# Weight sums of the seven-product pairs: made ahead and parked in DRAM, for 46 pairs instead of 33

## The chip, the cores and the metric

The kernel runs on one core of a Trainium2 chip. A core has TensorE (PE: matmuls; its weight loads are shown apart as PEld), VectorE (DVE), ScalarE (ACT), GpSimd (POOL) and SyncE (SP); DMA engines move data between DRAM and the on-chip memory, on queues that SP, ACT and POOL issue to. The metric is the device time of one execution in microseconds; lower is better.

## The reference

A trunk of two layers works on x of shape (1, 256, 2048) in float32: a gated linear attention layer, then a layer of block-sparse attention (with 256 positions and blocks of 256 each position sees its own block alone), and behind each a gated feed-forward block with a short convolution. The part around the change is the feed-forward block:

```python
def conv_ffn(x, norm_w, w_up, conv_w, conv_b, w_down):
    S = x.shape[1]
    h = rms_norm(x, norm_w) @ w_up                   # (256, 2048) @ (2048, 11264)
    hp = jnp.pad(h, ((0, 0), (CONV_WIDTH - 1, 0), (0, 0)))
    acc = conv_b
    for j in range(CONV_WIDTH):
        acc = acc + conv_w[j] * hp[:, j:j + S]
    a, u = jnp.split(acc, 2, axis=-1)
    return (jax.nn.silu(a) * u) @ w_down             # (256, 5632) @ (5632, 2048)

def reference(x, ...):
    h = x
    for layer in range(DEPTH):                       # 2
        h = h + (gla_mixer(h, ...) if layer < 1 else moba_mixer(h, ..., *shared_kv(h, ...)))
        h = h + conv_ffn(h, ...)
    return h
```

## The kernel before

**Products in three parts.** Matmuls run in a reduced float32 format. To keep the accuracy, every operand is split into a high part (a rounding copy by ACT, line 127 for weights) and a low part (the difference, by DVE, line 128), and a product is three matmuls: high x high, low x high, high x low.

**The weight stream.** `WeightStream` (lines 55 to 140) feeds all weights in the order in which they are used: chunks of 128 x 2048 float32 (1 MB) come by SP's queue into the pool `raw` (3 tiles, `wraw`), and each chunk is split in halves of 1024 columns (`whi`, `wlo`). Of four halves three live in the pool `parts` (3 tiles each) and, in most stages, the fourth in two *slots*. A slot is 4 KB per partition of the pool `big` (37 of them), which also holds h, the operands of the projections, the hidden activations (`hid`, 22 slots) and the combinations below. One `step()` of the program takes one half from the stream, after it has emitted the splits of the next three (two in the attention stage) and the loads up to three chunks ahead. `after(n, job)` puts a job n steps later.

**The stages** are: GLA with its output projection (128 steps), up projection 0 (176 steps), down projection 0, the attention stage with its output projection (128 steps), up projection 1 (176 steps) and down projection 1.

**The down projection.** `down` (lines 632 to 695) works on two blocks of 1024 output columns. A block takes 22 *pairs* of 128-row slices of w_down, each a 2 x 2 arrangement of tiles (2 row slices x 2 column halves of 512), against 2 x 2 tiles of the activations (2 row slices x 2 halves of the 256 positions). A plain pair makes all eight tile products, in two steps of 12 matmuls. A *seven* pair (marked + in `ORDERS`) uses the seven-product scheme for 2 x 2 matrices (Strassen's, in Winograd's form): it needs four sums of the pair's weight tiles and four sums of its activation tiles, and makes its products in four steps of 3, 6, 6 and 6 matmuls. The results of its extra products stand in four PSUM banks of their own and are drained into the outputs once for each block by `u_sums` (lines 697 to 718). The last pairs of each block, behind the last seven pair (`_tail`, up to three), are worked column half by column half.

The sums of the weights are made on the spot: `_sums` (lines 96 to 103) runs three DVE operations (lines 100 to 102) from the raw tile into the two slots `t13` and `t24`, and these are then split like any half. The sums of the activations are made by `combine` (lines 584 to 594) into one slot for each pair: for the pairs 1, 3, 5 and 7 (`EARLY`) during the up projection, for the others by `combine_parts` at the pairs 2, 4, 6 ... of the first block that uses them, and they serve both blocks.

Layer 0's second block also has jobs: two slots of h are loaded back at pairs 0 and 1, two more at 15 and 16 (`load_back`, POOL's queue), and at the pairs 2, 2, 3 and 4 the first block's outputs are turned on PE and added to h (`back`), followed at once by the work for the next norm (`nrm.feed`).

**What sets the order.** The program is written in one order; a planner at build time then orders each engine's and queue's instructions, by priority in the written order among those that its own costs hold to be ready, and hands out the tiles of each pool as they come free. On the chip each engine and each queue runs its list in that fixed order, waiting on semaphores.

## Time and profile before

| | before |
|---|---|
| median of 3 runs | 2219.98 us (2219.92 to 2220.67) |
| the profiled execution | 2220.21 us, of which the span of its instructions is 2218.4 |
| granted TensorE clock | 1.000 |
| busy: PE / PEld / DVE / ACT / POOL | 2212.0 / 1910.7 / 1669.9 / 1259.3 / 46.8 us |
| matmuls | 11781 |
| moved by DMA | 428.50 MB, mean 193 GB/s |
| down projection 0, 1 | 876.7 to 1106 us, 1986 to 2214 us of the span |

How to read it: the span is the time from the first to the last instruction. Busy time is the union of an engine's instructions. A matmul's own duration (390 ns for 512 columns) is longer than its distance from the next one, since matmuls are pipelined, so groups of matmuls that alternate are counted with overlap; stages are better compared by windows of time and by the distance of starts. In a group's row stand its line, engine and operation, out<-in, shapes, count, busy us, mean ns of one, and the idle time of the engine just before, with what ended it. In a row of waits stand who waited, for whom, us in total, how often, and the longest.

### The profile page before, as it was taken

The numbers are of one execution on the slowest core, as the hardware profiler recorded it, in microseconds if no ns is written. First come the engines' busy times: TensorE is split into PE (matmuls) and PEld (weight loads), VectorE is DVE, ScalarE is ACT, GpSimd is POOL, SyncE is SP. The second block draws the span as 40 slices with busy tenths as digits, with TensorE's granted clock in tenths as the row PEclk, the third lists the DMA queues.
The fourth block names the chain that finished last, engine by engine and source line by source line (L and its number), as shares of the span: only waits on it lengthen the run. The fifth ranks groups of instructions, "written<-read, shape, count | busy, mean of one in ns | idle before, by whom it ended". The sixth has DMA issues, their size and how long they took to land.

```text
span 2218.4 us, 30212 instructions
## 1 busy us (share of the span) xinstructions
PE 2212.0 (100%) x11781; PEld 1910.7 (86%) x11781; DVE 1669.9 (75%) x2291; ACT 1259.3 (57%) x1758; POOL 46.8 (2%) x61
## 2 busy tenths in 40 slices
PE   9999999999999999999999999999999999999999
PEld 7889888888888888888888888888888888888887
DVE  6666776788777778978866676567787777789896
ACT  6655644665555555645556665446555555556453
POOL 0000000000000000000010000000000000000000
PEclk9999999999999999999999999999999999999999
DMA  7554455555555555565655544555555555556664
GB/s 279 177 196 140 171 201 212 195 190 190 188 186 192 186 191 183 204 228 198 219 197 203 171 155 169 190 190 200 198 188 189 185 190 187 190 186 225 224 212 152
DMA packets 63442, 428.50 MB, mean 193 GB/s; under 512 B 7569, under 2 KB 8097, under 8 KB 13250
## 3 DMA queue, kind: packets, MB, share of 16 engines
q1 hardware_dynamic: 59490, 415.43, 53.7%
q0 software_dynamic: 3232, 10.56, 1.4%
q8 instruction: 92, 1.51, 0.3%
q10 hardware_dynamic: 576, 0.58, 0.1%
q14 instruction: 52, 0.43, 0.1%
HBM read 420.23 MB, written 6.32 MB: 192 GB/s over the span
## 4 chain that ended last, share of the span: by engine, by line
PE 99%; DMA 0%; ACT 0%; DVE 0%; SPq 0%; issue 0%
PE acc L312 40%; PE acc L314 21%; PE acc L662 13%; PE acc L327 10%; PE p L662 8%; PE acc L330 5%; PE sT L517 0%; DMA wraw<-w_v 0%; PE tr L855 0%; PE s L873 0%; PE pT L893 0%; PE z L423 0%; PE s L871 0%; PE oT L403 0%; PE o L403 0%; PE hT L726 0%
## 5 line engine op out<-in xcount | busy, mean ns | idle before, releaser
L127 ACT CAST whi<-wraw 128x1024 fp32r<-128x1024 f32 (+1 forms) x786 | 798.4, 1030 | 598.1 <-PE acc L312 329.1
L128 DVE TENSOR_TENSOR wlo<-wraw,whi 128x1024 fp32r<-128x1024 f32 (+1 forms) x786 | 926.8, 1195 | 260.6 <-ACT whi L127 135.5
L312 PE MATMUL acc<-xw,whi 128*128 128x512 f32 x3328 | 796.9, 391 | 0.0
L312 PEld LDWEIGHTS acc<-xw,whi 128*128 128x128 f32 x3328 | 610.9, 188 | 118.0
L314 PEld LDWEIGHTS acc<-xw,wlo 128*128 128x128 f32 x3328 | 426.8, 191 | 16.1
L314 PE MATMUL acc<-xw,wlo 128*128 128x256 f32 x3328 | 432.6, 283 | 0.0
L662 PE MATMUL acc<-whi,hid 128*128 128x512 f32 x572 | 181.9, 390 | 0.0
L662 PE MATMUL p<-whi,hid 128*128 128x512 f32 x506 | 164.6, 389 | 0.0
L327 PE MATMUL acc<-whi,xkv 128*128 128x512 f32 x512 | 133.6, 394 | 0.0
L327 PE MATMUL acc<-whi,xw 128*128 128x512 f32 x512 | 129.7, 393 | 1.1 <-ACT whi L127 1.1
L618 DVE SCALAR_TENSOR_TENSOR au<-up,cs,au 128x255 f32<-128x255 f32 x176 | 84.6, 482 | 59.4 <-ACT au L616 58.8
L662 PEld LDWEIGHTS acc<-whi,hid 128*128 128x128 f32 x572 | 107.0, 188 | 22.0
L340 ACT COPY up<-acc 128x512 f32<-128x512 f32 x88 | 51.6, 586 | 118.5 <-PE acc L314 117.9
L327 PEld LDWEIGHTS acc<-whi,xw 128*128 128x128 f32 x512 | 95.6, 189 | 21.9 <-ACT whi L127 2.0
L127 ACT CAST whi<-t 128x1024 fp32r<-128x1024 f32 x66 | 68.9, 1054 | 77.0 <-PE p L662 61.5
L662 PEld LDWEIGHTS p<-whi,hid 128*128 128x128 f32 x506 | 95.0, 188 | 19.8
L327 PEld LDWEIGHTS acc<-whi,xkv 128*128 128x128 f32 x512 | 94.3, 188 | 18.4
L616 ACT ACTIVATE au<-up,cs 128x256 f32<-128x256 f32 x176 | 96.0, 593 | 7.8 <-DVE up L612 7.8
L662 PE MATMUL acc<-wlo,hid 128*128 128x512 f32 x286 | 94.2, 389 | 0.0
L128 DVE TENSOR_TENSOR wlo<-t,whi 128x1024 fp32r<-128x1024 f32 x66 | 79.6, 1219 | 18.1 <-PE p L662 10.0
L662 PE MATMUL acc<-whi,comb 128*128 128x512 f32 x264 | 85.5, 389 | 0.0
L662 PE MATMUL p<-wlo,hid 128*128 128x512 f32 x253 | 83.4, 389 | 0.0
(259 smaller groups left out, 2027.7 us busy)
## 6 DMA issues: line engine op xcount, KB each, us to landing
wraw<-w_up SPq DMA_DIRECT2D x176, 1024.0 KB, 4.8
wraw<-w_dn SPq DMA_DIRECT2D x88, 1024.0 KB, 4.9
wraw<-w_g SPq DMA_DIRECT2D x16, 1024.0 KB, 4.9
wraw<-w_go SPq DMA_DIRECT2D x16, 1024.0 KB, 4.9
wraw<-w_mq SPq DMA_DIRECT2D x16, 1024.0 KB, 4.9
wraw<-w_kk SPq DMA_DIRECT2D x16, 1024.0 KB, 4.8
wraw<-w_kv SPq DMA_DIRECT2D x16, 1024.0 KB, 4.9
wraw<-w_mo SPq DMA_DIRECT2D x16, 1024.0 KB, 4.9
```

What stands on the lines that cost most here:

```text
L127: nc.scalar.copy(hi[:, a:b], src[:, a:b])
L128: nc.vector.tensor_sub(lo[:, a:b], src[:, a:b], hi[:, a:b].bitcast(F32))
L312: T.matmul(ps[:, b, :], two[i][0][:, c:c + 128], xs(kt), start=kt == 0, stop=False)
L314: T.matmul(ps[:, b, :S], two[i][1][:, c:c + 128], xs(kt)[:, :S], start=False, stop=kt == kts - 1)
L327: T.matmul(ps[:, t, :], xs(kt)[:, x0 + 128 * t:x0 + 128 * t + 128], hi[:, c:c + 512], start=kt == 0 and x0 == 0, stop=False)
L330: T.matmul(ps[:, t, :], xs(kt)[:, 128 * t:128 * t + 128], lo[:, c:c + 512], start=False, stop=kt == KT - 1)
L340: A.copy(t, ps[:, :, S:])
L616: A.activation(au[:, i, :], t[:, i, :], AF.Identity, bias=col(cb + n), scale=col(cw + 2 * 2 * FT + n))
L618: V.scalar_tensor_tensor(au[:, i, 1:], t[:, i, :S - 1], col(cw + 2 * FT + n), au[:, i, 1:], op0=OP.mult, op1=OP.add)
L662: T.matmul(p[n], x[xi], w[wi][:, 512 * f:512 * f + 512], start=n not in begun, stop=left[n] == 0)
```

## The change

- **More seven pairs.** `ORDERS` marks 11, 11, 11 and 13 pairs in the four blocks instead of 8, 8, 8 and 9, in a new order. A mark is now + or ^. Of the 46 marked pairs 23 carry each mark.
- **The weight sums are made ahead.** For every marked pair `make_ahead` loads the pair's four weight tiles once (1 MB, SP's queue, into a tile of `raw`), makes the four sums in place with four DVE operations of 128 x 512, one per step, 4 to 7 steps after the load, and stores the tile to DRAM by POOL's queue 8 steps after it. Layer 0's 22 pairs are made every 12 steps from step 24 of the program, layer 1's 24 pairs every 12 steps from the eighth step of the attention stage.
- **The stream loads them back.** A marked pair is now two chunks: the last three quarters of its weight tiles (in a new order, so that the one tile that is used alone comes first), and its parked sums. The sums of a + pair come into a `raw` tile, those of a ^ pair into two slots, in two transfers. `_sums` is gone. In the down projections the stream loads five chunks ahead instead of three.
- **Memory.** `raw` has 4 tiles instead of 3, `big` 35 slots instead of 37. `combine` packs the sums of four pairs' activations into three slots (the fourth sum of each pair goes into a part of `hid` that a seven pair doesn't use), and is called one pair earlier.
- **Order.** In a seven pair the products 6 and 5 share a step, and 7 and 4. In layer 0's second block both first reloads of h stand at pair 0, `back` at the pairs 2, 2, 3, 3, and `nrm.feed` apart from it at 4, 6, 8 and 10.

```diff
@@ -37,14 +37,15 @@
 def _order(text):
-    return [(int(k.rstrip("+")), k.endswith("+")) for k in text.split()]
+    return [(int(k.rstrip("+^")), k[len(k.rstrip("+^")):]) for k in text.split()]
 EARLY = (1, 3, 5, 7)
-ORDERS = [[_order("0 2 4 1+ 6 3+ 8 5+ 10 7+ 12 16 9+ 14 11+ 17 13+ 18 15+ 19 20 21"),
-           _order("0 2 4 6 8 1+ 10 3+ 12 5+ 14 7+ 16 9+ 17 11+ 18 13+ 19 15+ 20 21")],
-          [_order("0 2 4 1+ 6 3+ 8 5+ 10 7+ 12 16 9+ 14 11+ 17 13+ 18 15+ 19 20 21"),
-           _order("0 1+ 2 3+ 4 5+ 6 7+ 8 9+ 10 11+ 12 13+ 14 15+ 16 17+ 18 19 20 21")]]
+ORDERS = [[_order("0 1+ 2 3^ 4 5+ 6 7^ 8 9+ 11^ 10 13+ 15^ 12 16+ 17^ 14 19+ 18 20 21"),
+           _order("0 2 4 6 1+ 3^ 8 5+ 7^ 10 9+ 11^ 12 13+ 15^ 14 16+ 17^ 18 19+ 20 21")],
+          [_order("0 1+ 2 3^ 4 5+ 6 7^ 8 9+ 11^ 10 13+ 15^ 12 16+ 17^ 14 19+ 18 20 21"),
+           _order("0 1+ 2 3+ 5^ 4 7+ 9^ 6 11+ 13^ 8 15^ 16+ 10 17^ 19^ 18 12^ 14^ 20 21")]]
 def _tail(order):
@@ -63,61 +64,60 @@
         self.tiles, self.split = {}, {}
         self.n_dma = self.n_split = 0
         self.cuts, self.lead = {}, {}
-        self.sums, self.slot, self.first = {}, None, None
+        self.quads, self.slot, self.first = set(), None, None
+    def _chunk(self, rows, a, b, *halves, deep=True, slots=False):
+        self.halves += [(len(self.chunks), *half, deep) for half in halves]
+        self.chunks.append((rows, a, b, slots, len(self.halves) - 1))
+    @staticmethod
+    def rows(w, g, c0, n=2048):
+        return w[g, 128 * c0:128 * (c0 + n)].rearrange("(p c) -> p c", p=128)
...
+    def add_quads(self, w, g, order, parked):
         for i, (_, seven) in enumerate(order):
-            c = len(self.chunks)
-            self.halves += ([(c, 0, "b11"), (c, 1024, "wide"), (c, 0, "t13"), (c, 0, "t24")] if seven else
-                            [(c, 0, "wide"), (c, 1024, "wide")])
-            self.chunks.append((w, g, 2048 * i, 2048))
+            rows = self.rows(w, g, 2048 * i)
+            self.quads |= {len(self.chunks), len(self.chunks) + bool(seven)}
+            if seven:
+                self._chunk(rows, 512, 2048, (0, 512), (512, 1024))
+                self._chunk(parked[g, i], 0, 2048, (0, 1024), (1024, 1024), slots=seven == "^")
+            else:
+                self._chunk(rows, 0, 2048, (0, 1024), (1024, 1024))
     def _dma(self, upto):
         while self.n_dma < min(upto, len(self.chunks)):
-            w, g, c0, n = self.chunks[self.n_dma]
-            t = self.raw.tile([128, 2048], F32, name="wraw")
-            for a, b in self.cuts.get(self.n_dma, ((0, n),)):
-                rows = w[g, 128 * c0:128 * (c0 + n)].rearrange("(p c) -> p c", p=128)
-                self.nc.sync.dma_start(t[:, a:b], rows[:, a:b])
-                for job in self.lead.get((self.n_dma, a), ()):
-                    job()
+            rows, a0, b0, slots, _ = self.chunks[self.n_dma]
+            if slots:
+                t = [self.slot([128, 1024], F32, "sums") for _ in range(2)]
+                for i in range(2):
+                    self.nc.sync.dma_start(t[i], rows[:, 1024 * i:1024 * i + 1024])
+            else:
+                t = self.raw.tile([128, 2048], F32, name="wraw")
+                for a, b in self.cuts.get(self.n_dma, ((0, b0 - a0),)):
+                    self.nc.sync.dma_start(t[:, a:b], rows[:, a0 + a:a0 + b])
+                    for job in self.lead.get((self.n_dma, a), ()):
+                        job()
             self.tiles[self.n_dma] = t
             self.n_dma += 1
-    def _sums(self, c):
-        V, src = self.nc.vector, self.tiles[c]
-        t13, t24 = (self.slot([128, 1024], F32, k) for k in ("t13", "t24"))
-        V.tensor_sub(t13, src[:, 512:1536], src[:, 0:1024])
-        V.tensor_add(t24[:, :512], t13[:, 512:], src[:, :512])
-        V.tensor_sub(t24[:, 512:], src[:, 1536:], t24[:, :512])
-        self.sums[c] = {"t13": t13, "t24": t24}
     def prefetch(self, i):
         nc = self.nc
         while self.n_split < len(self.halves):
             n = self.n_split
-            c, o, kind = self.halves[n]
-            if n > i + self.AHEAD + (kind != "plain"):
+            c, o, width, deep = self.halves[n]
+            if n > i + self.AHEAD + deep:
                 break
             self._dma(c + 1)
-            for c_, _, kind_ in self.halves[n:n + 3]:
-                if kind_ == "b11" and c_ not in self.sums:
-                    self._dma(c_ + 1)
-                    self._sums(c_)
-            src = self.sums[c][kind] if kind in ("t13", "t24") else self.tiles[c][:, o:o + 1024]
-            if kind == "b11":
-                src = src[:, :512]
-            if kind != "plain" and n % 4 == 3:
+            t = self.tiles[c]
+            src = t[o // 1024] if isinstance(t, list) else t[:, o:o + width]
+            if deep and n % 4 == 3:
                 hi, lo = self.slot([128, 1024], F32R, "whi"), self.slot([128, 1024], F32R, "wlo")
             else:
                 hi = self.parts.tile([128, 1024], F32R, name="whi")
...
             self.split[n] = (hi, lo)
             self.n_split += 1
-            if kind == "t24":
-                del self.sums[c]
...
+            if self.chunks[c][-1] == n:
                 del self.tiles[c]
-                self._dma(c + 4)
+                self._dma(c + (6 if c in self.quads else 4))
...
@@ -147,8 +144,8 @@
-    big = ctx.enter_context(tc.tile_pool(name="big", bufs=37))
-    raw = ctx.enter_context(tc.tile_pool(name="raw", bufs=3))
+    big = ctx.enter_context(tc.tile_pool(name="big", bufs=35))
+    raw = ctx.enter_context(tc.tile_pool(name="raw", bufs=4))
     parts = ctx.enter_context(tc.tile_pool(name="parts", bufs=3))
     tmp = ctx.enter_context(tc.tile_pool(name="tmp", bufs=6))
     small = ctx.enter_context(tc.tile_pool(name="small", bufs=2))
@@ -166,6 +163,13 @@
         return mis_ps.tile(list(shape), F32, name=name, tag="bank")
 
     ws = WeightStream(tc, raw, parts)
+
+    ahead = [[(g, i) for g, order in enumerate(orders) for i, (_, seven) in enumerate(order) if seven]
+             for orders in ORDERS]
+    parked = []
+    for layer, todo in enumerate(ahead):
+        t = dram.tile([len(todo), 128, 2048], F32, name=f"tsum{layer}")
+        parked.append({at: t[n] for n, at in enumerate(todo)})
     plan = [(w_v2, 1, 16384), (w_v, 2, 8192), (w_k, 4, 4096), (w_qa, 4, 4096), (w_g, 8, 4096), (w_go, 8, 4096),
             (w_up0, FT, 4096), (w_dn0, 2, None),
             (w_mq, 4, 8192), (w_kk, 4, 8192), (w_kv, 4, 8192), (w_mo, 8, 4096),
...
@@ -292,6 +297,21 @@
 
     def after(steps, job):
         later.append((cur[0] + steps, job))
+
+    def make_ahead(layer, w, first, every):
+
+        def work(at):
+            t = raw.tile([128, 2048], F32, name="wraw")
+            b12, b11, b22, b21 = (t[:, 512 * i:512 * i + 512] for i in range(4))
+            jobs = [lambda: V.tensor_sub(b22, b22, b12), lambda: V.tensor_sub(b12, b12, b11),
+                    lambda: V.tensor_add(b11, b22, b11), lambda: V.tensor_sub(b21, b21, b11)]
+            nc.sync.dma_start(t, ws.rows(w, at[0], 2048 * at[1]))
+            for i, job in enumerate(jobs):
+                after(4 + i, job)
+            after(8, lambda: nc.gpsimd.dma_start(parked[layer][at], t))
+
+        for i, at in enumerate(ahead[layer]):
+            after(first + every * i, lambda at=at: work(at))
 
     def step(less=0):
         due = [job for at, job in later if at <= cur[0]]
@@ -373,6 +393,7 @@
+    make_ahead(0, w_dn0, 24, 12)
     nrm = Norm(C_GN, "xw", columns=True)
     for p in range(2):
         nrm.operand(p)
...
@@ -589,20 +610,31 @@
         V.tensor_sub(t[:, 1], t[:, 0], a0)
         V.tensor_sub(t[:, 2], a0, a1)
         V.tensor_sub(t[:, 3], b0, t[:, 1])
-        c = slot([128, 4, 2, 128], F32R, "comb")
-        split(c[:, :, 0], c[:, :, 1], t)
-        combos[k] = c
-
+        n = len(combos)
+        if n % 4 < 3:
+            rooms.append(slot([128, 4, 2, 128], F32R, "comb"))
+            c = rooms[-1]
+            split(c[:, 0:3, 0], c[:, 0:3, 1], t[:, 0:3])
+            combos[k] = [(c[:, f, 0], c[:, f, 1]) for f in range(3)]
+        else:
+            combos[k] = [(c[:, 3, 0], c[:, 3, 1]) for c in rooms[-3:]]
+            for f, parts_ in enumerate(combos[k]):
+                split(*parts_, t[:, f])
+        combos[k].append((hid_k[:, 0, 128:S], hid_k[:, 0, S + 128:]))
+        split(*combos[k][3], t[:, 3])
+
+    rooms = []
     combos = {}
 
     def combine_parts(k, hid):
         t = temp("whole")
         V.tensor_add(t, hid[k][:, :, :S], hid[k][:, :, S:])
-        combine(k, [(t[:, i, :128], t[:, i, 128:]) for i in range(2)])
+        combine(k, hid[k], [(t[:, i, :128], t[:, i, 128:]) for i in range(2)])
...
@@ -640,7 +672,7 @@
             done |= set(new)
             todo = dict(jobs.get(b, {}))
             for i, k in enumerate(new):
-                todo.setdefault(2 + 2 * i, []).append(late(k))
+                todo.setdefault(1 + 2 * i, []).append(late(k))
             low = acc_ps.tile([128, 2, 512], F32, name="acc")
             p = {2: low[:, 0], 3: low[:, 1], 4: bank("p4", (128, 512)), 8: bank("p8", (128, 512))}
             left = dict.fromkeys(range(1, 9), 0)
...
@@ -677,8 +709,8 @@
                 if seven:
                     prods((1, part(k, 0, 0), 0))
                     prods((3, comb(k, 3), 0), (2, part(k, 1, 0), 1))
-                    prods((5, comb(k, 0), 0), (7, comb(k, 2), 1))
-                    prods((6, comb(k, 1), 0), (4, part(k, 1, 1), 1))
+                    prods((6, comb(k, 1), 1), (5, comb(k, 0), 0))
+                    prods((7, comb(k, 2), 0), (4, part(k, 1, 1), 1))
                 else:
                     for a in range(2):
                         prods(*((n, part(k, a, t), f)
@@ -776,7 +808,6 @@
                     T.transpose(tp[:, i, 128 * t:128 * t + 128],
                                 r[2 * t + c][:, 128 * (i0 + i):128 * (i0 + i) + 128], ident)
             V.tensor_add(h[q], h[q], tp)
-            nrm.feed(q)
 
         def load_back(m):
             hs[m] = slot([128, 2, 2, S], F32, "h")
@@ -792,14 +823,19 @@
                 pair.extend(two[:, i].rearrange("p (a b) -> p a b", a=2) for i in range(2))
             return pair.pop(0)
 
-        jobs = {2: [lambda q=q: back(q, in_acc) for q in (0, 1)]}
-        for q, i in ((2, 3), (3, 4)):
-            jobs.setdefault(i, []).append(lambda q=q: back(q, in_acc))
-        for m, i in enumerate((0, 1, 15, 16)):
-            jobs.setdefault(i, []).append(lambda m=m: load_back(m))
+        jobs = {}
+        for i, job, n in ((0, load_back, 0), (0, load_back, 1), (2, back, 0), (2, back, 1), (3, back, 2), (3, back, 3),
+                          (4, nrm.feed, 0), (6, nrm.feed, 1), (8, nrm.feed, 2), (10, nrm.feed, 3),
+                          (15, load_back, 2), (16, load_back, 3)):
+            jobs.setdefault(i, []).append(lambda job=job, n=n: job(n, in_acc) if job is back else job(n))
         down(0, hid, ready, {1: jobs})
+
+        def last_back(q):
+            back(q, lambda: bank("hf", (128, 2, S)))
+            nrm.feed(q)
+
         for q in range(4, NP):
-            after(q - 3, lambda q=q: back(q, lambda: bank("hf", (128, 2, S))))
+            after(q - 3, lambda q=q: last_back(q))
         after(5, nrm.close)
 
     n_ffn = Norm(C_FN, "xw")
@@ -909,6 +945,7 @@
         ox.append(o)
 
     xkv = []
+    make_ahead(1, w_dn1, 8, 12)
     after(12, bias_rows)
     for p in range(NP):
         after(26 + p, lambda p=p: xkv.append(make_xw(p, C_KVN, "xkv")))
...
```

23 lines of the change are left out of this document (11 added, 12 removed).

## The prediction

> **What bounds the kernel now.** I read the page's busy shares first, then the chain that ended last, then the list of who waited for whom on PE, and last the busy time by stage.
>
> ```profile
> span 2218.4 us, 30212 instructions
> PE 2212.0 (100%) x11781; PEld 1910.7 (86%) x11781; DVE 1669.9 (75%) x2291; ACT 1259.3 (57%) x1758; POOL 46.8 (2%) x61
> PEclk9999999999999999999999999999999999999999
> DMA packets 63442, 428.50 MB, mean 193 GB/s; under 512 B 7569, under 2 KB 8097, under 8 KB 13250
> PE 99%; DMA 0%; ACT 0%; DVE 0%; SPq 0%; issue 0%
> ```
>
> The chain is 99% PE. A busy PE alone would prove little, since the ends of matmuls are modelled; what proves it is the whole list of PE's waits, and the spacing of matmuls inside the down projections, from pieces of the chain:
>
> ```profile
> engine line waited for: us in total, times, longest us
> PE junk L195 <- POOL idle L192: 1.3, 1, 1.3
> PE acc L327 <- ACT whi L127: 1.1, 2, 0.8
> ```
> ```profile
> 982.76 4.31 PE p L662 x19
> 987.07 4.53 PE acc L662 x20
> 2092.42 4.31 PE p L662 x19
> ```
>
> PE waits 2.4 us in the whole program, all in the first 14 us. In a down projection a matmul follows the last one every 4.31 / 19 = 0.227 us, at a granted clock of 9 tenths or more in every slice (1.00 in the stages below). So the down projections are a queue of matmuls with no hole in it: a matmul taken away is worth 0.227 us, and work taken from another engine there is worth nothing by itself. The stages (97 to 386 us: GLA; then up, down, attention, output and up, down) say how near the others are:
>
> ```profile
> 97.00:386.00 289.00, 289.00 (x1715) 257.31 (x1714) 197.90 (x266) 158.81 (x217) 4.78 (x8) 1.00 0.53 183
> 386.00:876.00 490.00, 490.00 (x2819) 433.05 (x2818) 379.44 (x551) 284.68 (x405) 0.54 (x1) 1.00 0.55 190
> 876.70:1106.00 229.30, 229.30 (x1021) 189.93 (x1020) 195.93 (x230) 124.13 (x141) 4.27 (x8) 1.00 0.59 208
> 1106.00:1401.00 295.00, 295.00 (x1431) 246.16 (x1430) 193.77 (x310) 175.84 (x300) 23.35 (x15) 1.00 0.52 178
> 1401.00:1986.00 585.00, 585.00 (x3381) 517.41 (x3380) 439.06 (x620) 332.70 (x471) 4.38 (x8) 1.00 0.56 192
> 1986.00:2214.00 228.00, 228.00 (x1010) 188.82 (x1008) 196.74 (x232) 118.69 (x130) 4.31 (x8) 1.00 0.57 204
> ```
>
> (Columns: window, its length, busy PE, PEld, DVE, ACT, POOL, granted clock, DMA share, GB/s.) VectorE is at 85 to 86% in both down stages, 66 to 77% elsewhere; the transfers stand under 0.6 everywhere.
>
> **Fewer matmuls.** A plain pair issues 2 steps of 12 matmuls, a pair with seven products 3 + 6 + 6 + 6 = 21. The orders hold 8 + 8 + 8 + 9 = 33 such pairs before and 11 + 11 + 11 + 13 = 46 after: 13 more, 39 matmuls fewer, 39 x 0.227 = 8.85 us. The new order of products inside a pair and of pairs in a block changes no count; transposes and drains stay. All of it lies on the path.
>
> **The sums on the spot go.** Their three rows, the copies and differences of the sums, and the costs that the 13 new pairs add:
>
> ```profile
> L100 DVE TENSOR_TENSOR t<-wraw 128x1024 f32<-128x1024 f32 x33 | 40.3, 1222 | 16.6 <-DMA wraw<-w_dn 16.3
> L101 DVE TENSOR_TENSOR t<-t,wraw 128x512 f32<-128x512 f32 x33 | 22.6, 684 | 0.1
> L102 DVE TENSOR_TENSOR t<-wraw,t 128x512 f32<-128x512 f32 x33 | 22.5, 683 | 0.1
> L128 DVE TENSOR_TENSOR wlo<-t,whi 128x1024 fp32r<-128x1024 f32 x66 | 79.6, 1219 | 18.1 <-PE p L662 10.0 <-ACT whi L127 7.8 <-PE acc L662 0.3
> L127 ACT CAST whi<-t 128x1024 fp32r<-128x1024 f32 x66 | 68.9, 1054 | 77.0 <-PE p L662 61.5 <-DVE t L102 10.1 <-DVE wlo L128 2.7
> L128 DVE TENSOR_TENSOR wlo<-wraw,whi 128x512 fp32r<-128x512 f32 x37 | 25.2, 684 | 2.3 <-ACT whi L127 2.3
> L127 ACT CAST whi<-wraw 128x512 fp32r<-128x512 f32 x37 | 22.9, 621 | 28.4 <-PE acc L662 13.3 <-PE p L662 10.8 <-DMA wraw<-w_v 2.8
> L600 DVE TENSOR_TENSOR whole<-hid 128x512 f32<-128x512 f32 x9 | 6.1, 683 | 0.0
> ```
>
> VectorE loses 33 x (1.222 + 0.684 + 0.683) = 85.4 us in the down stages. The 13 new pairs split 3584 columns where a plain pair splits 2048, so each adds one long and one short split: 13 x (1.219 + 0.684) = 24.7 us on VectorE, 13 x (1.054 + 0.621) = 21.8 us on ScalarE. Activation sums made late go from 9 to 16 (layer 0: 7, layer 1: 9); each costs a whole (0.68), four small operations and the splits, some 2.5 us: 17.5 us. VectorE in the two down stages falls from 393 to about 393 - 85 + 25 + 17 = 350 us of 448. That is relief, priced at nothing, because PE was not waiting for it.
>
> **The sums ahead arrive elsewhere.** 46 times a raw tile is loaded (1 MB, SP queue), four 128x512 operations run on VectorE at 0.684 us (L101's duration), and 1 MB is stored by POOL's queue. 46 x 2.74 = 125.9 us of VectorE, spread at one sum per 12 steps. 12 steps are 6 chunks of two steps; layer 0's up stage (490 us, 176 steps) gives 2.78 us a step, 33.4 us a sum, so VectorE there goes from 77% by 2.74 / 33.4 = 8 points to 86%. The cover is the lead of the splits:
>
> ```profile
> DVE wlo L128 <- PE acc L314: 94.7, 73, 5.2
> ```
> ```profile
> ACT whi L127 <- PE acc L312: 329.1, 202, 4.8
> ACT whi L127 <- DMA wraw<-w_dn: 28.1, 16, 6.7
> ```
>
> VectorE and ScalarE wait for PE to give buffers back, up to 5.2 and 4.8 us at a time: they run ahead. An operation of 0.68 us fits into that. Bounds: if nothing of the 125.9 us is hidden, the kernel ends at 2337; if all is, zero. I take zero, the end that PE's wait list lies at; should the cover go, the splits of the next step would be late.
>
> POOL's queue gains 46 issues of 0.54 us (the row of hspill below), ahead of the small powers in the attention stage and of the parked and reloaded h; POOL is busy 23 of 295 us there. A store that waits for VectorE's fourth operation holds up what is behind it on POOL, a power for instance, and VectorE's product that waits for the power; the lag is that of one operation, 0.7 us, under the same lead of the splits, and priced at nothing.
>
> **Transfers.** Traffic grows by 46 x 3 x 1.049 MB, less 46 x 0.262 MB for the quarter that a pair no longer loads: 132.7 MB, 428.5 to 561 MB, 254 GB/s over the span.
>
> ```profile
> q1 hardware_dynamic: 59490, 415.43, 53.7%
> wraw<-w_dn SPq DMA_DIRECT2D x88, 1024.0 KB, 4.9
> hspill<-h POOLq DMA_DIRECT2D x8, 256.0 KB, 4.2
> ```
> ```profile
> 7.00:17.00 10.00, 8.90 (x37) 6.70 (x37) 7.37 (x12) 8.68 (x16) 0.00 (x0) 1.00 1.02 406
> ```
> ```profile
> L755 POOL DMA_DIRECT2D hspill<-h x8: 539/540/574, 316.0 to 388.7; - x8
> ```
>
> In a down projection a pair with sums now loads 1.835 MB in 21 x 0.227 = 4.77 us (385 GB/s), a plain pair 1.049 MB in 5.45 us; two of the first and one of the second, the densest pattern, take 15.0 us for 4.72 MB, 315 GB/s. The start of this program moved 406 GB/s for 10 us, all engines busy, so both figures are under what the transfers have shown. Between a raw tile's release and the use of its next content lie three other raw chunks (four tiles), 9.5 us (a double ahead of a plain chunk) to 13 us here, against 4.9 to land. Priced at zero; the bound above is rival A.
>
> **Steps that move.** In layer 0's second block both reloads of h (4 issues of POOL) stand at pair 0, the turning back of h at pairs 2, 2, 3, 3 instead of 2, 2, 3, 4, and the four feeds (two casts, a square, their differences and a sum, 2.3 us of VectorE) come apart from it, at pairs 4, 6, 8 and 10.
>
> ```profile
> L778 DVE TENSOR_TENSOR h<-h,acc 128x512 f32<-128x512 f32 x4 | 2.7, 683 | 3.1 <-PE acc L776 3.1
> L785 POOL DMA_DIRECT2D h<-hspill x8: 536/537/543, 972.4 to 1055.5; - x8
> ```
>
> The first seven pair now comes at pair 4, not 5, and takes the two PSUM tiles that the turned h leaves; the last two additions (0.683 each) have half a pair, 2.7 us, and VectorE gets them before later splits. Nothing charged; if late, PE waits once, for 1 to 3 us. In the last block the tail shrinks from 3 pairs to 2: the drain of the eight sums, some 9 operations of 0.68 us, lies beside 48 matmuls (10.9 us) and stays covered; what follows the last matmul is as before.
>
> **Slots and tiles.** Two slots of 37 go, one raw tile comes. Counting allocations in the order of the program: before, at most 36 of 37 live; after, 35 of 35 at the end of the up stages and in the second half of each first block (22 activations, 9 combination slots, 2 of a split, 2 of loaded sums). The split that uses slots then starts only when the one four steps earlier is used up, with three steps (15 matmuls, 3.4 us) to make 1.054 + 1.219 us. It fits by 1.1 us; with two other splits (1.219 each) in front on VectorE 1.3 us are missing, at some 8 such places 10 us. Ends 0 and 10; I take 0, since the ordinary buffers live by the same three steps today with no wait on PE. A load of sums that waits for two slots holds up the raw loads behind it on SP's queue: in the second block of layer 0 the count asks for 36 at the second pair, so that load waits out one pair, 5.45 us, with some 9 steps (over 20 us) left until its use. The fourth raw tile lets the fourth chunk load earlier at the start, where PE is busy 8.90 of 10 us: at best it takes away that 1.1 us, at worst delays what is ahead as much.
>
> **Sum.** The profiled execution took 2220.21 us, 1.8 more than its span, and lies 0.23 above the median of three. 2220.21 - 8.85 = 2211.4; from the median 2211.1. I say 2211.3.
>
> **Rivals.**
> A, late weights, on the other side: the transfers do not sustain 385 GB/s and the lead of three tiles is used up. At the 354 GB/s of a rougher stretch
>
> ```profile
> 4.00:14.00 10.00, 8.90 (x31) 6.24 (x30) 5.94 (x11) 6.94 (x13) 1.71 (x5) 1.00 0.94 354
> ```
>
> a double (3.67 MB) takes 10.37 us instead of 9.54; with 3 + 5 + 3 + 6 = 17 doubles in the four blocks, 14.1 us lost: 2225.5. It decides against the change from 0.78 us per double on. For it: ScalarE already waits 28.1 us for w_dn. Against: a double and its plain pair need 4.72 MB / 354 = 13.3 us of transfers in 15.0, so the plain pair refills the lead. 0.12.
>
> The Trainium skill's page "DMA: Bandwidth & Descriptors", section "Specifications", gives a limit of about 358 GB/s from HBM for one core; the 406 over 10 us lie above it, so the measurement decides. By the page's figure a double would need 10.25 us, an estimate, and the 17 of them with no lead would lose 12 us, for 2223: rival A again.
>
> B, the sums ahead disturb: VectorE, in order, stands at the first operation until its 1 MB has landed, with the splits behind it; or the load waits for a raw tile. At 0.1 us lost per sum 2215.9; from 0.29 us on slower. For it: VectorE does wait for tiles today, 16.3 us at L100. Against: four steps, 11 us, between load and use, 4.9 to land. 0.20, mostly 2213 to 2217.
>
> C, PE is not the limit, so 39 matmuls fewer change nothing: 2220. Against: PE's wait list. The Trainium skill's page "Perfetto Trace Analysis", section "Identifying the Most-Contended Engine", holds matmul occupancy to be a bad measure and LDWEIGHTS occupancy a good one; that stands at 86% here, so by that rule PE has room and something else sets the pace. The even 0.227 us speaks against it, and against this rival. 0.04.
>
> **How the numbers follow.** All hidden, 0.64: 2211.3, between 2209.8 (the start's 1.1 us gained) and 2213. With most of B the range reaches 2217. 0.2% of 2220, 4.4 us, is about what a measurement here can tell from no change: faster means under 2215.5, slower over 2224.4. Faster: 0.64 and 0.14 of B, 0.78. Same: C and 0.05 of B, 0.09. Slower: A and 0.01 of B, 0.13.
>
> **What would show it.** Right: PE's wait list still only a few us, 11742 matmuls, the down stages some 225.2 and 223.2 us long (18 and 21 matmuls fewer), VectorE near 350 us in them and 85% in the up stages, 560 MB. Wrong by A: PE waits for whi behind wraw or sums in the second half of a block; by B: PE waits at L312 or L327 every 12 steps; by slots: waits of ScalarE for PE with PE then waiting for whi around the 13th to 16th pair of a first block.

## The result, and the profile after

Seven runs of the changed kernel have a median of 2213.23 us (2211.97 to 2213.68), seven of the kernel before, taken beside them, 2220.18 us (2219.74 to 2220.67). The ratio is 0.9966, 95% interval 0.9955 to 0.9978: some 7 us faster, of the 8.85 that 39 matmuls are worth. The runs do not scatter evenly: three lie at 2211.97 to 2212.11, four at 2213.23 to 2213.68. The profiled execution took 2212.01 us and is one of the lower three, so what follows explains 8.2 us out of the span (2218.4 to 2210.2); the further 1.3 us of the upper four need other evidence.

The page of the changed kernel, with the counts and the chain, then the list of PE's waits (who waited for whom, us in total, times, longest):

```profile
span 2210.2 us, 30840 instructions
PE 2203.1 (100%) x11742; PEld 1902.4 (86%) x11742; DVE 1731.5 (78%) x2478; ACT 1292.6 (58%) x1825; POOL 69.5 (3%) x107
DMA packets 86631, 561.20 MB, mean 254 GB/s; under 512 B 10145, under 2 KB 10673, under 8 KB 27602
PE 98%; DMA 1%; DVE 1%; ACT 0%; issue 0%; SPq 0%; ACTq 0%; DVEq 0%
```
```profile
PE acc L347 <- ACT whi L127: 1.6, 2, 0.8
PE junk L200 <- POOL idle L197: 1.3, 1, 1.3
PE acc L694 <- DVE wlo L128: 0.3, 2, 0.2
```

The matmuls are 39 fewer, PE is still the chain, and it still waits for nearly nothing. Two things are new. DMA and VectorE each stand in the chain with 1%, and PE's list has a row in the down projections (L694), where it had none: two waits for the low halves (wlo) that VectorE makes.

The stages again, in the columns of the prediction (window, length, busy PE, PEld, DVE, ACT, POOL, granted clock, DMA share, GB/s), GLA to the second down projection:

```profile
97.00:386.00 289.00, 289.00 (x1715) 257.27 (x1714) 217.75 (x298) 159.35 (x218) 9.03 (x16) 1.00 0.68 244
386.00:876.00 490.00, 490.00 (x2819) 433.03 (x2819) 405.66 (x609) 287.26 (x411) 7.47 (x14) 1.00 0.69 247
876.70:1102.00 225.30, 225.12 (x1002) 186.13 (x1001) 176.51 (x220) 136.50 (x165) 4.27 (x8) 1.00 0.81 290
1102.00:1397.00 295.00, 295.00 (x1432) 246.08 (x1431) 209.89 (x342) 175.91 (x300) 25.84 (x23) 1.00 0.65 230
1397.00:1982.00 585.00, 585.00 (x3381) 517.37 (x3380) 473.93 (x692) 336.62 (x477) 12.86 (x24) 1.00 0.71 251
1982.00:2206.00 224.00, 223.82 (x991) 185.09 (x990) 179.46 (x232) 133.48 (x161) 4.32 (x8) 1.00 0.80 289
```

VectorE's work has moved out of the down projections into the other stages, and the transfers now stand at 0.80 of the DMA engines in the down projections, where it was 0.57 to 0.59. Only there do PE's 225.12 of 225.30 and 223.82 of 224.00 us show holes.

The timeline of the first hole (start, duration, engine, line; in brackets the idle time before):

```profile
908.40 1.06 ACT L127 CAST whi<-wraw 128x1024 fp32r<-128x1024 f32 x1 [1.90 <-PE acc L694]
908.42 0.28 DVE L373 TENSOR_TENSOR comb<-comb 128x128 fp32r<-128x128 f32 x1
...
908.62 1.22 DVE L128 TENSOR_TENSOR wlo<-wraw,whi 128x1024 fp32r<-128x1024 f32 x1
...
909.10 0.61 PE L694 MATMUL p<-whi,hid 128*128 128x512 f32 x2
909.75 0.28 DVE L609 TENSOR_TENSOR comb<-whole 128x128 f32<-128x128 f32 x1
909.89 0.30 PEld L694 LDWEIGHTS acc<-wlo,hid 128*128 128x128 f32 x2 [0.60 <-DVE wlo L128]
909.89 0.73 PE L694 MATMUL acc<-wlo,hid 128*128 128x512 f32 x2 [0.17 <-DVE wlo L128]
```

VectorE makes the wlo that PE needs from 908.62 to 909.84, directly behind a small operation of the late activation sums (L373), and the next one (L609) follows it; eight more operations of these sums stand between the splits of the 6 us before, without a pause on VectorE. By the starts of the matmuls, one comes 563 ns after the one before, here (from 909.33) and at the same place of layer 1 (from 2015.33), instead of 227 ns, and the next one another 336 ns later. That is 0.34 + 0.11 us at each place, 0.89 in all. (The list of waits has 0.2 for each, since it counts from the modelled end of a matmul, 390 ns after its start, and only idle time over 0.15 us.)

The lengths of the two down projections agree with that. From the start of the first to the start of the last matmul of L662 (L694 after) they fell from 232.45 to 228.83 us and from 227.60 to 223.31. The 18 and 21 matmuls fewer are worth 4.09 and 4.77 us; less 0.45 for each stall, 3.64 and 4.32; measured 3.63 and 4.29. The other 0.25 of the 8.18 us by which the span fell lies outside the down projections, most of it behind the last of these matmuls.

### The profile page after: what moved, and what is told of

Same layout as the page of the kernel before. It is cut to its first block, busy times and chain, and to the rows that moved or that the text cites. A ratio compares the mean times of both kernels' runs of the same rounds, so it can differ in the third digit from the quotient of the medians.

```text
span 2210.2 us, 30840 instructions
## 1 busy us (share of the span) xinstructions
PE 2203.1 (100%) x11742; PEld 1902.4 (86%) x11742; DVE 1731.5 (78%) x2478; ACT 1292.6 (58%) x1825; POOL 69.5 (3%) x107
## 4 chain that ended last, share of the span: by engine, by line
PE 98%; DMA 1%; DVE 1%; ACT 0%; issue 0%; SPq 0%; ACTq 0%; DVEq 0%
PE acc L332 40%; PE acc L334 21%; PE acc L694 13%; PE acc L347 10%; PE p L694 6%; PE acc L350 5%; PE sT L538 0%; DVE wlo L128 0%; DMA wraw<-w_v 0%; PE tr L891 0%; ACT whi L127 0%; PE s L909 0%; DMA wraw<-w_dn 0%; PE pT L929 0%; PE z L444 0%; PE oT L424 0%
## 5 line engine op out<-in xcount | busy, mean ns | idle before, releaser
L127 ACT CAST whi<-wraw 128x1024 fp32r<-128x1024 f32 (+1 forms) x832 | 839.5, 1024 | 604.9 <-PE acc L332 319.1
L128 DVE TENSOR_TENSOR wlo<-wraw,whi 128x1024 fp32r<-128x1024 f32 (+1 forms) x832 | 973.0, 1188 | 273.7 <-ACT whi L127 155.3
L694 PE MATMUL acc<-whi,hid 128*128 128x512 f32 x612 | 183.5, 390 | 0.0
L694 PE MATMUL p<-whi,hid 128*128 128x512 f32 x428 | 139.4, 389 | 0.0
L694 PEld LDWEIGHTS acc<-whi,hid 128*128 128x128 f32 x612 | 114.6, 188 | 23.6
L347 PE MATMUL acc<-whi,xkv 128*128 128x512 f32 x512 | 134.5, 394 | 0.0
L347 PE MATMUL acc<-whi,xw 128*128 128x512 f32 x512 | 129.0, 392 | 1.6 <-ACT whi L127 1.6
L347 PEld LDWEIGHTS acc<-whi,xw 128*128 128x128 f32 x512 | 95.3, 188 | 22.5 <-ACT whi L127 2.5
L347 PEld LDWEIGHTS acc<-whi,xkv 128*128 128x128 f32 x512 | 93.7, 188 | 17.8
L694 PE MATMUL acc<-wlo,hid 128*128 128x512 f32 x306 | 100.1, 390 | 0.3 <-DVE wlo L128 0.3
L694 PEld LDWEIGHTS p<-whi,hid 128*128 128x128 f32 x428 | 80.3, 188 | 16.8
L694 PE MATMUL acc<-whi,comb 128*128 128x512 f32 x276 | 83.0, 389 | 0.0
L652 DVE SCALAR_TENSOR_TENSOR au<-up,cs,au 128x254 f32<-128x254 f32 x176 | 80.9, 476 | 0.0
L694 PE MATMUL p<-wlo,hid 128*128 128x512 f32 x214 | 70.9, 389 | 0.0
L350 PE MATMUL acc<-wlo,xkv 128*128 128x512 f32 x256 | 69.8, 391 | 0.0
```

What stands on the lines that cost most here:

```text
L127: nc.scalar.copy(hi[:, a:b], src[:, a:b])
L128: nc.vector.tensor_sub(lo[:, a:b], src[:, a:b], hi[:, a:b].bitcast(F32))
L347: T.matmul(ps[:, t, :], xs(kt)[:, x0 + 128 * t:x0 + 128 * t + 128], hi[:, c:c + 512], start=kt == 0 and x0 == 0, stop=False)
L350: T.matmul(ps[:, t, :], xs(kt)[:, 128 * t:128 * t + 128], lo[:, c:c + 512], start=False, stop=kt == KT - 1)
L652: V.scalar_tensor_tensor(au[:, i, 2:], t[:, i, :S - 2], col(cw + n), au[:, i, 2:], op0=OP.mult, op1=OP.add)
L694: T.matmul(p[n], x[xi], w[wi][:, 512 * f:512 * f + 512], start=n not in begun, stop=left[n] == 0)
```

## The experiments

Each stands beside runs of the kernel before on the same chip, whose medians lay between 2219.9 and 2220.2; the ratios are to these. Line numbers of the kernel before differ (its L662 is L694 here). Where a wait of PE is placed in time, the time is the start of the matmul before it.

**The changed kernel with the old number of pairs.** Sums made ahead, parked, half in slots, but the orders of the kernel before, 33 pairs.

```diff
-ORDERS = [[_order("0 1+ 2 3^ 4 5+ 6 7^ 8 9+ 11^ 10 13+ 15^ 12 16+ 17^ 14 19+ 18 20 21"),
+ORDERS = [[_order("0 2 4 1+ 6 3^ 8 5+ 10 7^ 12 16 9+ 14 11^ 17 13+ 18 15^ 19 20 21"),
...
```

> The changed kernel with the 33 marked pairs of before (every second one with its sums in slots): all else as changed, sums still made ahead. Theory (the count of matmuls is all that pays): 39 matmuls come back, 8.85 us, so 2220 to 2222. Rival (VectorE's relief from the sums on the spot pays by itself): under 2219.

Measured 2220.01 us (2219.47 to 2220.16), ratio 1.0000, interval 0.9991 to 1.0009. Everything but the number of pairs is worth nothing that shows: neither does the relief of VectorE in the down projections pay, nor does making ahead cost. Two effects that cancel are unlikely: its list of PE's waits has no row in the down projections, and the kernel before has none there either, so there was no wait for the relief to take away.

**The old kernel with 46 pairs.** Sums on the spot, as before, with the new orders (every mark a +).

```diff
-ORDERS = [[_order("0 2 4 1+ 6 3+ 8 5+ 10 7+ 12 16 9+ 14 11+ 17 13+ 18 15+ 19 20 21"),
+ORDERS = [[_order("0 1+ 2 3+ 4 5+ 6 7+ 8 9+ 11+ 10 13+ 15+ 12 16+ 17+ 14 19+ 18 20 21"),
...
```

> The kernel before with the changed orders: 46 marked pairs, sums made on the spot by three VectorE operations each. Theory (the gain needs the sums made elsewhere): VectorE needs 350 us + 46 x 2.59 us = 469 us in down stages of 449 us, so PE waits 20 us or more in all: 2231 to 2245, with PE waiting for wlo in the list of waits. Rival (only the count matters, the sums on the spot were hidden and would stay so): 2211 to 2213.

Measured 2229.63 us (2228.75 to 2230.15), ratio 1.0043, interval 1.0030 to 1.0056: 9.6 us slower than before with 39 matmuls fewer, and 16 to 17 us slower than the changed kernel. The direction is the theory's; the time lies just under its range. Its waits of PE, and its two down projections:

```profile
PE acc L662 <- ACT whi L127: 6.3, 8, 1.9
PE acc L662 <- DVE wlo L128: 2.2, 5, 0.8
```
```profile
877.00:1110.00 233.00, 227.41 (x993) 183.34 (x992) 220.89 (x273) 134.10 (x155) 4.25 (x8) 1.00 0.59 203
1986.00:2214.00 228.00, 224.70 (x981) 182.96 (x980) 226.20 (x285) 132.07 (x150) 4.29 (x8) 0.99 0.59 203
```

VectorE is busy 220.89 of 233 and 226.20 of 228 us: it has become the limit there, and PE has holes. Most of PE's waits are for the high halves, which ScalarE makes; what ScalarE waits for in the first down projection says why, this kernel first, the kernel before second:

```profile
ACT whi L127 <- DVE t L102: 34.7, 15, 4.8
ACT whi L127 <- DMA wraw<-w_dn: 3.1, 5, 1.2
```
```profile
ACT whi L127 <- DMA wraw<-w_dn: 16.2, 6, 6.7
ACT whi L127 <- DVE t L102: 5.6, 6, 1.7
```

ScalarE waits for VectorE's sums (L102), and less than before for weights to land, so late loads are not the cause. The relief, worth nothing with 33 pairs, is what makes room for 46. That is the use of making ahead: the moved VectorE work is not itself a gain, it is the condition of one.

**Making ahead alone.** The kernel before, with 46 sums made and parked as in the changed kernel, and none used.

```diff
+    make_ahead(0, w_dn0, 24, 12)
...
+    make_ahead(1, w_dn1, 8, 12)
```

> The kernel before, with 33 marked pairs and sums on the spot, that also makes 46 sums ahead and parks them (22 in layer 0, 24 in layer 1) and never reads them; raw has 4 tiles, big 35 slots. Theory (making ahead is hidden): 2220 to 2222. Rival B (making ahead disturbs, 0.1 us or more per sum): 2224.8 or more.

Measured 2220.80 us (2220.26 to 2221.27), ratio 1.0003, interval 0.9995 to 1.0012. The 184 operations on VectorE (126 us by their durations; its busy time rises by 99.4, as neighbouring operations overlap in the record) and the 96 MB of loads and stores cost 0.8 us by the medians; the interval holds anything from nothing to 2.7. In the first up projection VectorE is as busy as in the changed kernel, and PE is busy without a break:

```profile
386.00:876.00 490.00, 490.00 (x2819) 433.06 (x2818) 405.05 (x603) 287.63 (x405) 7.47 (x14) 1.00 0.70 248
```

**Loading without making.** The changed kernel without make_ahead; what stood for the sums is loaded from the pair's own weights, in the same amounts and to the same tiles (so what it computes is another).

```diff
-                self._chunk(parked[g, i], 0, 2048, (0, 1024), (1024, 1024), slots=seven == "^")
+                self._chunk(rows, 0, 2048, (0, 1024), (1024, 1024), slots=seven == "^")
...
-    make_ahead(0, w_dn0, 24, 12)
```

> The changed kernel without making sums ahead: in the place of the parked sums it loads the pair's own four weight tiles, the same 1 MB on the same queue in the same shapes, so the down projections compute with unsummed tiles and the output is another. Theory (making ahead is hidden): 2211 to 2213.5, the two groups of times of the changed kernel (near 2212.0 and near 2213.4) both still there. Rival B (the second group comes from the traffic or the VectorE work of making ahead): all runs at 2212.0 or under.

Measured 2212.83 us (2212.40 to 2214.30), ratio 0.9970, interval 0.9958 to 0.9981, the same as the changed kernel: rival B falls, as no time lies at 2212.0 or under. Its profile fell on a time of 2214.02 us, and shows what the profile of the changed kernel does not:

```profile
PE acc L693 <- ACT whi L127: 1.2, 3, 0.7
PE acc L693 <- DVE wlo L128: 0.2, 1, 0.2
```

Three waits of PE for the high halves, at 1081.69, 2114.35 and 2120.37 us, all in second blocks. The making ahead has no part in them, as it is not there.

**The changed kernel again.**

> The changed kernel as it is, for more times and a second profile. Its times fall near 2212.0 or near 2213.4. Theory (late weights, rival A in small): an execution of the upper group shows PE waiting for a copy of ScalarE that waited for a w_dn or tsum load, in a second block of a down projection, 0.5 to 1.2 us in all. Rival: the upper group has its 1.3 us at the start of the program, or everywhere.

Measured 2212.32 us (2212.14 to 2213.45), ratio 0.9967, interval 0.9955 to 0.9979; four of its six times lie at 2212.1 to 2212.3, two at 2213.4. The profile (2212.22 us) is again one of the lower ones and shows the same two waits for wlo, at 908.88 and 2015.39. By the starts of the matmuls it also loses 0.4 us at 1067 and 1082, before matmuls with high halves, too little at a time for the list of waits. No profile shows an upper time of this very kernel, so the expectation stays open.

**All parked sums through the raw tiles, none through slots.** Each ^ becomes +.

```diff
-ORDERS = [[_order("0 1+ 2 3^ 4 5+ 6 7^ 8 9+ 11^ 10 13+ 15^ 12 16+ 17^ 14 19+ 18 20 21"),
+ORDERS = [[_order("0 1+ 2 3+ 4 5+ 6 7+ 8 9+ 11+ 10 13+ 15+ 12 16+ 17+ 14 19+ 18 20 21"),
...
```

> The changed kernel with every mark a +: all sums come into raw tiles, none into slots. In two marked pairs in a row three raw chunks then hold 2.04 + 2.73 + 2.04 = 6.8 us of matmuls, against some 6 us to land. Theory (the lead of the loads is what runs short): PE waits for ScalarE behind wraw, 2215 to 2225. Rival (the lead is ample, as the prediction priced it): 2212 to 2213.7.

Measured 2218.83 us (2215.01 to 2223.30), ratio 0.9993, interval 0.9984 to 1.0002. All but 1 us of the gain is gone by the median, with the same matmuls. ScalarE's waits in the first down projection, then PE's, of this kernel:

```profile
ACT whi L127 <- DMA wraw<-w_dn: 25.6, 17, 3.3
ACT whi L127 <- DMA wraw<-tsum: 15.2, 9, 2.8
```
```profile
PE acc L694 <- ACT whi L127: 2.5, 3, 1.2
PE acc L347 <- ACT whi L127: 2.0, 1, 2.0
PE acc L694 <- DVE wlo L128: 0.7, 3, 0.2
```

and the rows of the changed kernel that answer to the first two:

```profile
ACT whi L127 <- DMA wraw<-w_dn: 7.6, 6, 2.1
ACT whi L127 <- DMA wraw<-tsum: 1.2, 2, 0.8
```

The copies wait over four times as long for data to land (40.8 us against 8.8), and PE begins to wait for the copies. So the lead of the loads (how far ahead of their use they can start), not their rate, is what is scarce: slots let a load start while the raw tiles are still full. Not all of the loss is that. The span of this profile is 7.5 us longer than the changed kernel's. By the starts of the matmuls 2.5 of them arise in the first 18 us of the program, long before a parked sum is used: PE waits 2.0 us at L347, and behind it the granted clock was 0.57 from 14 to 18 us (1.00 in the changed kernel), with matmuls 427 ns apart instead of 227. The other 5.0 us lie in the second blocks of the two down projections.

**More traffic in the down projections.** A marked pair loads its whole 1 MB of weights instead of 768 KB.

```diff
-                self._chunk(rows, 512, 2048, (0, 512), (512, 1024))
+                self._chunk(rows, 0, 2048, (512, 512), (1024, 1024))
```

> The changed kernel, but a marked pair loads all four of its weight tiles (1 MB) though it uses three quarters: 12.1 MB more, all in the down projections, 440 GB/s instead of 385 in two marked pairs in a row, 350 instead of 315 with the plain pair behind. Theory (transfers of the down projections are at their margin): 2214 to 2219, the wait at ScalarE's copies. Rival (they are well under what the queue delivers): 2212 to 2213.7.

Measured 2213.38 us (2212.05 to 2215.79), ratio 0.9971, interval 0.9959 to 0.9982: 1.1 us more than the changed kernel on the same chip (2212.32), 0.2 more than in its first runs, no difference that is clear of the scatter. One time, 2215.79, lies above the rival's range. The profile (2213.60 us) has one wait of 1.0 us for whi, at 2115.39, and rates of 400 GB/s there:

```profile
2106.00:2116.00 10.00, 9.78 (x44) 7.76 (x42) 4.68 (x6) 2.79 (x4) 0.00 (x0) 1.00 1.01 400
```

In the changed kernel the same stretch is as full, without a hole in PE:

```profile
2106.00:2116.00 10.00, 10.00 (x46) 8.27 (x45) 4.89 (x6) 4.57 (x6) 0.00 (x0) 1.00 1.01 411
```

**The late activation sums one pair later.**

```diff
-                todo.setdefault(1 + 2 * i, []).append(late(k))
+                todo.setdefault(2 + 2 * i, []).append(late(k))
```

> The changed kernel with the late activation sums called at pairs 2, 4, 6 ... as before, not 1, 3, 5. In the changed kernel PE waits for VectorE's wlo once in each layer's first block (909.9 us and its like in layer 1, some 0.34 us each), where small operations of these sums stand in front of it. Theory: called later they are out of the way there, the two waits go, 0.7 us less. Rival (they are only pushed to another pair, or stand in the planner's order anyway): no change, or waits at other places.

Measured 2211.19 us (2210.56 to 2213.14), ratio 0.9962, interval 0.9950 to 0.9975. Both waits for wlo are gone; the profile (2210.56 us) has these alone:

```profile
PE junk L200 <- POOL idle L197: 1.3, 1, 1.3
PE acc L347 <- ACT whi L127: 0.5, 1, 0.5
```

From their first to their last matmul the two down projections are 228.46 and 222.84 us long, 0.83 us less together than in the changed kernel, close to the 0.89 above (the recorded 0.34 each leaves out the second late matmul). So these stalls hung on the place of the sums: the same operations, one pair later, cause none. Two of the five times still lie at 2212.8 and 2213.1.

**The output stores of the first block on POOL's queue.** At the start of the last block, SP's queue stands at stores that wait for VectorE, and loads of weights are queued behind them. The edit takes the stores away from there.

```diff
-                    (A if n == 8 else nc.sync).dma_start(out[t, :, c0:c0 + 512], x)
+                    (A if n == 8 else nc.sync if b else nc.gpsimd).dma_start(out[t, :, c0:c0 + 512], x)
```

> Only the queue of the four output stores that follow layer 1's first down block is changed, from SP to POOL. Theory (the loads of weights behind these stores on SP's queue wait with them for VectorE, and where they then land a little late PE waits 0.5 to 1.4 us at the fourth to sixth pair of the last block): the loads of the last block are issued earlier, the stretch from 2106 to 2116 us no longer has all DMA engines busy, and the times lie at 2212.0 without those near 2213.4; the two waits of 0.34 us for wlo in the first blocks stay. Rival (the late weights come from the density of loads alone, or from layer 0's second block as well): PE's waits stay and the times still spread from 2212.0 to 2213.7. Second rival: the stores now stand on POOL's queue ahead of the loads of the second block's h, which come late, and PE waits for the sums with h: over 2214.

Measured 2212.83 us (2211.81 to 2213.77), ratio 0.9967, interval 0.9955 to 0.9980. The theory falls: the spread is as before, and the profile (2213.77 us) has PE waiting for whi at 2114.04, near the waits of the run that loads without making (2114.35) and of the one with more traffic (2115.39). SP's waits from 2060 to 2130 us tell why, the changed kernel first, this one second:

```profile
SPq L104 <- DVE wlo L128: 42.9, 16, 8.3
SPq L778 <- DVE res L776: 8.5, 3, 6.9
```
```profile
SPq L104 <- DVE wlo L128: 43.6, 16, 8.2
SPq L104 <- DVE hid L373: 7.8, 1, 7.8
```

The 6.9 us in which a store (L778) held the queue are now 7.8 us in which the load behind it (L104) waits itself. The release that ends it is VectorE's, by the list an operation of the late activation sums; the load needs a raw tile, and none is free any earlier. It is issued at 2100.35 us in the changed kernel and at 2100.23 here. The store had stood in front of a load that could not have started.

**Both edits.**

> The stores moved to POOL's queue and the late activation sums moved by one step (2 + 2i). Theory: the two effects lie at different places and add: 2212.0 - 0.67 = 2211.3 at the most, 2210.6 as the run with the later sums alone had at its least, with no times near 2213. Rival (the spread comes from elsewhere): 2210.6 to 2213.1, as with the later sums alone.

Measured 2211.47 us (2211.31 to 2212.92), ratio 0.9962, interval 0.9949 to 0.9976: the gain of the later sums, and none that shows of the moved stores, as the rival had it; one of the five times is still 2212.92.

**49 pairs.** Both edits, and pair 18 with seven products in three more blocks (with a new order in layer 0's second block); a sum every 11 steps.

```diff
-ORDERS = [[_order("0 1+ 2 3^ 4 5+ 6 7^ 8 9+ 11^ 10 13+ 15^ 12 16+ 17^ 14 19+ 18 20 21"),
+ORDERS = [[_order("0 1+ 2 3^ 4 5+ 6 7^ 8 9+ 11^ 10 13+ 15^ 12 16+ 17^ 14 19+ 18^ 20 21"),
...
-    make_ahead(0, w_dn0, 24, 12)
+    make_ahead(0, w_dn0, 24, 11)
```

> As the run with both edits, with 49 pairs of seven products in place of 46 (12 + 12 + 12 + 13; pair 18 with slots added in three blocks, one sum made every 11 steps). Theory (each pair is worth 3 x 0.227 = 0.68 us until the lead of the loads or VectorE runs short): 3 x 0.68 = 2.0 us under the run with both edits, 2208.6 to 2209.3. Rival (the lead is at its end with 46 pairs, as the run without slots hints): late weights in the second blocks or late activation sums take back 2 us or more, 2210.5 to 2214.

Measured 2210.39 us (2210.25 to 2210.50), ratio 0.9956, interval 0.9943 to 0.9968. Pair 18 of the last block here takes activations that its own sums have partly overwritten, so the output is another. With pairs 12 and 18 exchanged there:

```diff
-           _order("0 1+ 2 3+ 5^ 4 7+ 9^ 6 11+ 13^ 8 15^ 16+ 10 17^ 19^ 18 12^ 14^ 20 21")]]
+           _order("0 1+ 2 3+ 5^ 4 7+ 9^ 6 11+ 13^ 8 15^ 16+ 10 17^ 19^ 12 18^ 14^ 20 21")]]
```

> As the run with 49 pairs, with pairs 12 and 18 of the last block exchanged: pair 18, whose activation sums stand there from the first block, takes seven products, and pair 12 stays plain. (In the run before, pair 18 was plain in the last block though a quarter of its activations had been overwritten by its own sums in the first, so its output was another; the work was the same.) Kinds of pairs, places and loads are the same; one combination less is made in the last block. Theory: the time of that run, 2210.4, between 2209.9 and 2210.9, the 49 pairs keeping about 1.1 of the 2.0 us that nine matmuls fewer are worth beside the run with both edits (2211.5). Rival (that run's time hung on its order in the last block): 2211.3 to 2213, no better than 46 pairs.

Measured 2210.46 us (2209.93 to 2211.38), ratio 0.9957, interval 0.9944 to 0.9971. Its page and PE's waits:

```profile
span 2209.2 us, 30905 instructions
PE 2202.5 (100%) x11733; PEld 1901.1 (86%) x11733; DVE 1744.9 (79%) x2505; ACT 1294.9 (59%) x1835; POOL 75.7 (3%) x113
```
```profile
PE acc L347 <- ACT whi L127: 1.1, 2, 0.9
PE acc L694 <- DVE wlo L128: 0.4, 2, 0.2
```

Nine matmuls fewer are worth 2.04 us; by the medians 0.7 to 1.0 are kept, against the two runs with the later sums and 46 pairs (2211.19 and 2211.47). There are waits for wlo again, at 1044.17 and 1045.35, but of another origin: they lie in layer 0's second block, where no late activation sums are made. There ScalarE waits 3.2 us, until 1037.6, for a w_dn load, VectorE waits 2.9 us for ScalarE and then runs without a pause. By the starts of the matmuls 1.5 us are lost from 1038 to 1046, as much as the six matmuls that layer 0 saves (1.36); layer 1's down projection is 0.66 us shorter than in the run with the later sums alone, what its three matmuls are worth (0.68). The intervals of the ratios overlap, so the step from 46 to 49 alone isn't settled. That this version beats both kernels is: all its times lie under the least of the thirteen of the changed kernel (2211.97).

## Why the prediction was right, and what it left out

The forecast of 2211.3 us was met within about 1 us by the lower times, and within 2 us by the median. That median, 2213.23, lies 0.2 us above the 2213 that the prediction gave the case with all hidden, inside the wider range that it held open for rival B. There the room was luck, as the runs speak against B; what lengthened the runs were terms priced at nothing, the late activation sums and, probably, the transfers. (The median of all thirteen times of the changed kernel, 2212.33, needs no such room.)

**Fewer matmuls, 39 x 0.227 = 8.85 us: right, in mechanism and size.** With 33 pairs all else is worth 0.0 us; with 46 the two down projections became shorter by 8.85 us less the two stalls. Inside a down projection a matmul still follows every 0.227 us (4.99 / 22), in the chain of the changed kernel:

```profile
985.44 4.99 PE acc L694 x22
```

**The sums on the spot, worth nothing by themselves: right.** VectorE has 176.51 + 179.46 = 356 us in the down projections, 350 predicted. What the step did not say is that without this relief the 46 pairs cost 9.6 us, since VectorE, busy 447 of 461 us, makes the sums late, and with them both halves that PE needs.

**Making ahead, hidden: right.** VectorE reached 83% in layer 0's up stage (405.66 of 490) and 81% in layer 1's (with the output projection before it), 85% predicted, and the price was 0.8 us by the medians of the run that makes them alone, nothing that shows in the two others. Rival B falls. The slots were rightly priced at 0 too: in neither profile of the changed kernel does PE wait at the 13th to 16th pair of a first block. The fourth raw tile took nothing off the start: PE waits 1.6 and 1.4 us there in the two profiles, 1.1 before.

**Activation sums made late, priced at nothing: a term that was mis-sized, 0.89 us.** The step counted them as part of a sum of busy time (393 to 350 us) and never looked at where they stand. A busy share that falls over a stage says nothing of one split that is late in it; the order of the operations ahead of each split on VectorE has to be looked at for that.

**Transfers priced at zero: right for the lower times, probably short by 1.3 us for the upper ones.** Wherever a profile of these variants fell on an upper time (2213.60, 2213.77, 2214.02), PE waits for high halves whose copies wait for weights, and by the starts of the matmuls 1.1 to 1.3 us are lost from 2114 to 2121 us alone; the last down projection is 224.6 to 224.8 us long from first to last matmul, and 223.3 in the changed kernel's profile. In the profiles from 2210.56 to 2212.22 of the variants with 46 pairs and slots that wait is absent, at 2211.38 it is 0.2 us, at another place (1081). This is rival A's mechanism at a tenth of its price, at a few places (at 902 and 1081 us too in some profiles) and not in 17 doubles. That it explains the upper times of the changed kernel itself is inferred from its variants, not shown in it; what makes the weights land later in one execution than in the next stays open. The stores ahead of them on SP's queue are not it.

**Rival A's price and rival C.** The prediction's argument against A was that a plain pair refills the lead. It held on the whole, as 256 KB more per pair cost 1.1 us at most by the medians. But it compared rates, and the run without slots shows that the lead decides: same bytes, 5 us more in the down projections. Rival C, PE not the limit, falls with the first experiment and the changed kernel together. The Trainium skill's page "Perfetto Trace Analysis", section "Identifying the Most-Contended Engine", would judge how much room PE has by its share of peak work and the busy share of LDWEIGHTS, not by matmul busy time. That share reads 86% in every kernel here but the one with 46 sums on the spot (85%), also where each matmul removed paid in full. In the down projections of the kernel before it even puts VectorE first (195.93 us against 189.93, of 229.30), whose relief was worth nothing. So in this case the distance of starts decided.

## What to carry to other kernels

Read the value of removed work from the spacing of the instructions on the engine that bounds the stage, and treat relief of another engine as the condition of a further step and not as a gain: here it was worth 0.0 us alone, and 13 more pairs came out 16 to 17 us faster with it than without. Then go through the order on the engines that feed the bound one, since a few small operations ahead of an urgent split, at one place in each layer, cost 0.89 us under a mean load of 80%. Where loads wait for buffers, count the room they can start into before the bytes: fewer rooms cost 5 us here, 256 KB more per pair at most 1.1. And an instruction that blocks a queue costs nothing if the one behind it could not have started either.

## What the runs showed that was not expected

The transfers of this one core ran at 400 to 411 GB/s for 10 us with all DMA engines busy (share 1.01), in the rows above, and at 425 in the run that loads without making:

```profile
2106.00:2116.00 10.00, 9.81 (x44) 7.81 (x43) 4.69 (x6) 3.90 (x6) 0.00 (x0) 1.00 1.03 425
```

The Trainium skill's page "DMA: Bandwidth & Descriptors", section "Bandwidth", measured 425 GB/s for a 16 MB transfer of a core alone. The runs agree with that figure, and not with the limit of about 358 that the prediction quoted from "Specifications".

Behind some waits PE ran slower for a few us. In the run with all sums through raw tiles it was from 14 to 18 us, as told above; in the old kernel with 46 pairs, behind a wait of 1.9 us at 2020, the granted clock was 0.70 and 0.50 in the next two stretches of 2 us, with matmuls 427 ns apart. An equally long wait of the same run, at 905 us, had no such thing behind it (clock 1.00), so the runs give no rule.

A blocked queue can be innocent: taking the stores off it turned 6.9 us of their wait into 7.8 us of the next load's, and moved the time by nothing.
